# Start addresses of the buffers that TensorE reads: multiples of 256 bytes, and weight buffers 4128 bytes apart

## The chip, the cores and the metric
The kernel runs on one core of one Trainium2 chip. The metric is the device time of one execution in microseconds (us), of which the median of three runs is shown. A NeuronCore has TensorE (PE: matmuls, with a separate queue of weight loads, PEld), VectorE (DVE), ScalarE (ACT), GpSimd (POOL) and SyncE (SP, which here issues all the DMAs). On-chip memory (SBUF) has 128 partitions; an address below is a byte offset within each partition.

## The reference
Two layers on 256 tokens of width 1024, in fp32. A layer is a token mixer and a feed-forward block, each followed by a LayerNorm of `alpha * x + f(x)`.

```
proj = x @ w_in                      # x_rnn | g_rnn | q latent | kv latent | rope key | gate A | gate B
y_rnn = gelu(g_rnn) * rg_lru(causal_conv4(x_rnn))
y_mla = 16-head causal attention from the low-rank latents
x = layer_norm(alpha*x + (sigmoid(gateA)*y_rnn + sigmoid(gateB)*y_mla) @ w_out)
h_gate, h_val = split(causal_conv3(x @ w_up))          # 2 * 3072 columns
x = layer_norm(alpha*x + (gelu(h_gate) * h_val) @ w_down)
```

## The kernel before, in words
**Products.** A float32 matrix is split into a high part (`hi`, rounded to the type float32r by ScalarE, line 182) and a low rest (`lo`, the difference, by VectorE, line 183). `mm3` (lines 190 to 193) then makes one product of three matmuls: hi by hi, hi by lo, lo by hi. Each matmul has a stationary operand, brought in by a weight load of 128 columns (512 bytes per partition), and a moving operand, which streams through.

**Who is stationary and who moves.** In `proj_pair` (lines 515 to 528; all of x @ w_in but the latents, and x @ w_up from the third pair of columns on) the weights `wh`, `wl` are stationary and the activations `xhi`, `xlo` move, 256 columns (1024 bytes) at a time; 48 matmuls make one pair. `qps`, `kps`, `peps` and `gates` have the same shape and stationary `wh`, `wl`; the moving operand of `gates` are the tiles `xch`, `xcl`. In the down projection (`out_chunk` into `dacc`) and the output projection (into `oacc`) it is the other way round: activations (`hh`, `hl`; `mhi`, `mlo`) are stationary, weights (`wsh`, `wsl`; `wh`, `wl`) move, 512 columns at a time.

**Buffers.** `wpool` has 4 buffers `raw` of 8192 bytes, which the DMAs fill, and 6 each of `wh` and `wl` of 4096 bytes; `load_split` takes two of each per load, in rotation, so that successive loads use buffers 0 and 1, 2 and 3, 4 and 5. `big` has 19 buffers of 4096 bytes (`slot`), among them `xhi`, `xlo`, `mhi`, `mlo`, and the weights `wsh`, `wsl` of `load_split` with `in_slots`; and 4 of the residual. `sm` has 13 buffers of 1024 bytes (tag `k1`: `xch`, `xcl`, `hh`, `hl` and others) and 7 of 1536 (tag `k15`: the scores and the conv outputs), and small ones for statistics.

**Addresses.** Buffers are placed one after the other, pool by pool, at multiples of 32 bytes. By the allocated program `raw`, `wh`, `wl`, all slots and the residuals start 192 bytes past a multiple of 256; the `k1` tiles start on one; `k15` starts 96 past one, and the identity 128 past one. Slices used as operands start at further multiples of 512 bytes, but for the latent weights' second half (64 past one).

**Order.** The order on TensorE is written out: `ORDER` (lines 43 to 49) for the mixer, and the loops of `up` and `out_chunk` for the feed-forward, in which one `proj_pair` of 48 matmuls and one chunk of the down projection of 12 take turns. The other engines' order comes from a planner with issue-order edges (`behind`).

Of the kernel before, what the change touches and what calls it, by code (L numbers as in the profile page):

```python
# [11 lines left out]
F32 = mybir.dt.float32  # L12
# [5 lines left out]
P = 128  # L18
# [30 lines left out]
)  # L49
HELD = 4  # L50
WARM = 8
KORD = (0, 1, 4, 5, 2, 3, 6, 7)
NPAIR = DFF // P
ALPHA = (2 * DEPTH) ** 0.25
# [69 lines left out]
def trunk(ctx, tc, x_tok, x_chan, pos, wts, par, lnrow, consts, out):  # L124
# [4 lines left out]
    T = nc.tensor  # L129

    cpool = ctx.enter_context(tc.tile_pool(name="cpool", bufs=1))
    wpool = ctx.enter_context(tc.tile_pool(name="wpool", bufs=1))
    big = ctx.enter_context(tc.tile_pool(name="big", bufs=1))
    sm = ctx.enter_context(tc.tile_pool(name="sm", bufs=2))
    pp = ctx.enter_context(tc.tile_pool(name="pp", bufs=4, space=bass.MemoryType.PSUM))

    def slot(name, dt=F32):
        return big.tile([P, 1024], dt, tag="t4", name=name, bufs=19)

    def bank(name):  # L140
        return pp.tile([P, 512], F32, tag="pb", name=name)
# [3 lines left out]

    def load_raw(l, key, parts=None, between=None):
        o, n = WOFF[key]
        raw = wpool.tile([P, 2048], F32, tag="raw", name=f"raw{l}", bufs=4)
        src = wts[l, o:o + P * n].rearrange("(p n) -> p n", p=P)
        for i, (a, b) in enumerate(parts or ((0, n),)):  # L150
            if between and b == n:
                between()
            nc.sync.dma_start(out=raw[:, a:b], in_=src[:, a:b])
        return raw
# [11 lines left out]
    def load_split(l, key, cuts, in_slots=False, after=(None, None),  # L166
                   step=1024, parts=None, between=None):
        raw = load_raw(l, key, parts, between)
        if later[0]:
            after = ready[0]  # L170
        n = WOFF[key][1]
        res = []
        for a, b in cuts:
            if in_slots:
                hi, lo = slot("wsh", F32R), slot("wsl", F32R)
            else:
                hi = wpool.tile([P, 1024], F32R, tag="wh", name="wh", bufs=6)
                lo = wpool.tile([P, 1024], F32R, tag="wl", name="wl", bufs=6)
            for c in range(a, b, step):
                d = min(c + step, b)  # L180
                h, w = hi[:, c - a:d - a], raw[:, c:d]
                behind(A.activation(h, w, AF.Copy), after[0])  # L182
                lo_ins = V.tensor_tensor(out=lo[:, c - a:d - a], in0=w, in1=h.bitcast(F32),  # L183
                                         op=ALU.subtract)
                behind(lo_ins, after[1])
                last_split[0] = lo_ins
            res.append((hi, lo))
        return res
# [10 lines left out]
    ctx.enter_context(tc.manual_schedule(engines={mybir.EngineType.PE}))  # L199


    idle = cpool.tile([P, P], F32, name="idle")
    V.memset(idle, 0.0)
    spare = bank("spare")
    for _ in range(WARM):
# [26 lines left out]
        latw0.update(latent_weights(0, i, step=LATW if i > 1 else LH,  # L232
                                    parts=((0, LATW), (LATW, 2 * LATW))))

    ident = cpool.tile([P, P], F32, name="ident")
    make_identity(nc, ident)
    mask = cpool.tile([P, 2 * P], F32, name="mask")
    G.memset(mask, 0.0)
# [8 lines left out]
    for l in range(DEPTH):  # L247
# [3 lines left out]
    posi = cpool.tile([P, S], I32, name="posi")  # L251
    nc.sync.dma_start(out=posi, in_=pos[0:1, :].to_broadcast([P, S]))
    xres = [
        big.tile([P, D], F32, tag="xres", name=f"xres{t}", bufs=4) for t in range(NT)
    ]

    def pcol(l, name, i, n=1):
# [117 lines left out]
    class LayerNorm:  # L375
# [12 lines left out]

        def tile(self, t, accs):
            l, last = self.l, self.last  # L390
            z = big.tile([P, D], F32, tag="xres", name="z", bufs=4)
            st = sm.tile([P, 2, 6], F32, tag="st", name="st")
            mv = sm.tile([P, 2], F32, tag="mv", name="mv")
            rs = sm.tile([P, 1], F32, tag="rs", name="rs")
            hs = [slice(512 * h, 512 * h + 512) for h in range(2)]
            for h in range(2):
                V.scalar_tensor_tensor(
                    out=z[:, hs[h]], in0=self.xres[t][:, hs[h]], scalar=ALPHA, in1=accs[t][h],
                    op0=ALU.mult, op1=ALU.add,
                )  # L400
                V.bn_stats(st[:, h], z[:, hs[h]])
            V.bn_aggr(mv, st.rearrange("p a b -> p (a b)"))
            V.tensor_scalar(out=rs, in0=mv[:, 1:2], scalar1=EPS, scalar2=None, op0=ALU.add)
            G.tensor_tensor(out=rs, in0=rs, in1=nhalf[:, 0:1], op=ALU.pow)
            g, b = self.gb
            if last:
                for h in range(2):
                    V.scalar_tensor_tensor(out=z[:, hs[h]], in0=z[:, hs[h]], scalar=mv[:, 0:1],
                                           in1=g[:, hs[h]], op0=ALU.subtract, op1=ALU.mult)
                for h in range(2):  # L410
                    V.scalar_tensor_tensor(out=z[:, hs[h]], in0=z[:, hs[h]], scalar=rs,
                                           in1=b[:, hs[h]], op0=ALU.mult, op1=ALU.add)
                    nc.sync.dma_start(out=out[t * P:(t + 1) * P, hs[h]], in_=z[:, hs[h]])
                return
            nmr = sm.tile([P, 1], F32, tag="nmr", name="nmr")
            V.scalar_tensor_tensor(out=nmr, in0=mv[:, 0:1], scalar=-1.0, in1=rs,
                                   op0=ALU.mult, op1=ALU.mult)
            for c in (0, 256):
                V.tensor_scalar(out=z[:, c:c + 256], in0=z[:, c:c + 256], scalar1=mv[:, 0:1],
                                scalar2=rs, op0=ALU.subtract, op1=ALU.mult)  # L420
            A.activation(z[:, hs[1]], z[:, hs[1]], AF.Identity, scale=rs, bias=nmr)
            self.res.append(z)

        def turn(self, t):
# [8 lines left out]
            for cc in range(2):  # L433
                for q in range(2):
                    hi, lo = (v.rearrange("p (c s) -> p c s", c=4) for v in self.xs[q])
                    xt = sm.tile([P, 2, P], F32, tag="k1", name="lnx", bufs=13)
                    hv, lv = hi[:, 2 * cc:2 * cc + 2, ts], lo[:, 2 * cc:2 * cc + 2, ts]
                    for e in range(2):
                        c = 2 * cc + e
                        gc = pcol(l, self.gn, 4 * q + c)  # L440
                        bc = pcol(l, self.bn, 4 * q + c)
                        src = pts[q][:, c * P:(c + 1) * P]
                        if q == 0:
                            V.tensor_scalar(out=xt[:, e], in0=src, scalar1=gc, scalar2=bc,
                                            op0=ALU.mult, op1=ALU.add)
                        else:
                            behind(A.activation(xt[:, e], src, AF.Identity, scale=gc, bias=bc),
                                   ea)
                    ea = A.activation(hv, xt, AF.Copy)
                    ev = V.tensor_tensor(out=lv, in0=xt, in1=hv.bitcast(F32), op=ALU.subtract)  # L450
# [30 lines left out]
    def lat_evac(l, t):  # L481
# [2 lines left out]
            A.activation(lt[:, h * LH:(h + 1) * LH], lacc[t][h][:, :LH], AF.Copy)  # L484
        lat.append(lt)
        sq = slot("sq")
        ms = sm.tile([P, 2], F32, tag="ms", name="ms")
        A.activation(sq[:, :QL], lt[:, :QL], AF.Square, scale=QL ** -0.5,
                     accum_out=ms[:, 0:1])
        A.activation(sq[:, QL:QL + KVL], lt[:, QL:QL + KVL], AF.Square,  # L490
# [17 lines left out]
    for l in range(DEPTH):  # L508
# [83 lines left out]
        def conv_branch(i):  # L592
            ps = proj_pair(("x", i))
            for m in range(2):
# [5 lines left out]
                for k in range(1, 4):  # L600
# [1 line left out]
                        out=dst[:, k:], in0=src[:, :S - k], scalar=pcol(l, "cw", 8 * (3 - k) + c),  # L602
                        in1=dst[:, k:], op0=ALU.mult, op1=ALU.add,
                    ))
                xh = sm.tile([P, S], F32R, tag="k1", name="xch", bufs=13)
                xl = sm.tile([P, S], F32R, tag="k1", name="xcl", bufs=13)
                A.activation(xh, dst, AF.Copy)
                V.tensor_tensor(out=xl, in0=dst, in1=xh.bitcast(F32), op=ALU.subtract)
                xsp[c] = (xh, xl)
# [136 lines left out]
        def scores(c):  # L746
            g, pr = divmod(c, 2)
            _, q96, k96 = qk[g]
            rsum = sm.tile([P, 2, 2], F32, tag="rsum", name="rsum", bufs=3)
            sns = []  # L750
            for hh in range(2):
                h4 = 2 * pr + hh
# [2 lines left out]
                         start=True, stop=True)  # L755
                T.matmul(sps[:, P:P + S], lhsT=q96[:, h4, P:], rhs=k96[:, h4],  # L756
                         start=True, stop=True)
                sn = sm.tile([P, 3 * P], F32, tag="k15", name="sn", bufs=7)
                nm = sm.tile([P, 2], F32, tag="nm", name="nm", bufs=4)
                V.tensor_tensor_reduce(sn[:, :P], sps[:, :P], mask[:, P:], -1.0, 3e38,  # L760
                                       ALU.add, ALU.min, nm[:, 0:1])
                er = V.tensor_tensor_reduce(sn[:, P:], sps[:, P:3 * P], mask, -1.0, 3e38,
# [14 lines left out]
        def flip(c):  # L777
            sns = pst[c]
            pts = []
            for hh in range(2):  # L780
                ptp = bank("ptp")
                for b in range(3):
                    T.transpose(ptp[:, b * P:(b + 1) * P], sns[hh][:, b * P:(b + 1) * P], ident)  # L783
                pT = sm.tile([P, 3 * P], F32, tag="k15", name="pT", bufs=7)
                A.activation(pT, ptp[:, :3 * P], AF.Copy)
                pts.append(pT)
            pst[c] = pts

        def values(c):
# [10 lines left out]
            if mer[c // 4] is None:  # L800
                mer[c // 4] = (slot("mhi", F32R), slot("mlo", F32R))
            cs = slice((c % 4) * S, (c % 4) * S + S)
            mg = sm.tile([P, S], F32, tag="k1", name="mg", bufs=13)
            V.tensor_tensor(out=mg, in0=yps[:, :S], in1=sB[c // 4][:, cs], op=ALU.mult)
            V.tensor_tensor(out=mg, in0=mg, in1=r_t[c // 4][:, cs], op=ALU.add)
            split2(mer[c // 4][0][:, cs], mer[c // 4][1][:, cs], mg)
# [76 lines left out]
        def up(j):  # L883
# [8 lines left out]
            for m in range(2):  # L892
                ch = m * NPAIR + j
                src = ps[:, m * S:(m + 1) * S]
                dst = sm.tile([P, S], F32, tag="k15", name=f"u{m}", bufs=7)
                ea = A.activation(dst, src, AF.Identity, scale=pcol(l, "fw", 96 + ch),  # L896
                                  bias=pcol(l, "fb", ch))
                for k in range(1, 3):
# [6 lines left out]
            convs.append((ea, ev))  # L905
            A.activation(u[0], u[0], AF.Gelu_apprx_tanh)
            V.tensor_tensor(out=u[1], in0=u[1], in1=u[0], op=ALU.mult)  # L907
            mh = sm.tile([P, S], F32R, tag="k1", name="hh", bufs=13)
            ml = sm.tile([P, S], F32R, tag="k1", name="hl", bufs=13)
            split2(mh, ml, u[1])  # L910
            hq[j] = (mh, ml)

# [145 lines left out]
```

## Time and profile before
| | |
|---|---|
| median of 3 runs | 804.9 us (804.83 to 805.35) |
| profiled execution, its own time | 804.24 us |
| its span, first to last instruction | 802.4 us |
| mean granted TensorE clock | 0.997 of full |
| busy: PE, PEld, DVE, ACT | 791.0, 741.2, 650.5, 509.1 us |

The span is that of one execution. A matmul's listed duration includes the time that it takes to pass through the array and overlaps its successors, so busy times of PE say little; the distance from one matmul's start to the next one's (its pitch below) is what a stream of them costs. Start times in the timeline are given to 0.01 us, so a pitch is read over many matmuls.

### The profile page before, as it was taken

What the parts mean: (1) busy time and instruction counts of PE and PEld (TensorE: products, weight loads), DVE (VectorE), ACT (ScalarE), POOL (GpSimd) and SP (SyncE); (2) the same over time, 40 slices, a digit from 0 to 9 for tenths busy, and PEclk for the clock granted to TensorE, in tenths of its full rate; (3) what the DMA queues carried; (4) which work ended last, traced back from release to release, by engine and by line L of the source; (5) the groups of instructions that cost most, each with busy time, mean ns of one, the idle gap of its engine ahead of it and who ended that gap; (6) DMA issues with size and microseconds to landing.
All of it is one profiled execution on the core that took longest, in us unless ns stands there. A gap on an engine that the chain in (4) does not pass through costs nothing.

```text
span 802.4 us, 14518 instructions
## 1 busy us (share of the span) xinstructions
PE 791.0 (99%) x5712; PEld 741.2 (92%) x5712; DVE 650.5 (81%) x1260; ACT 509.1 (63%) x910; POOL 10.9 (1%) x27
## 2 busy tenths in 40 slices
PE   9999999999999999999999999999999999999996
PEld 8999899878999999999899999998799999999994
DVE  6998889997699977667777886999887998677755
ACT  5765987783777465556475579688567665555540
POOL 1000000000000000000000000000000000000000
PEclk9999999999999999999999999999999999999998
DMA  8955436524356655435625544563524756655311
GB/s 313 344 185 211 152 115 242 187 85 181 158 210 263 210 177 209 174 122 218 236 79 201 183 169 139 173 219 121 208 76 184 276 196 211 210 165 203 106 53 53
DMA packets 26468, 144.76 MB, mean 180 GB/s; under 512 B 3360, under 2 KB 7072, under 8 KB 11808
## 3 DMA queue, kind: packets, MB, share of 16 engines
q1 hardware_dynamic: 26400, 143.84, 50.6%
q8 instruction: 45, 0.74, 0.4%
q14 instruction: 23, 0.19, 0.1%
HBM read 140.68 MB, written 1.05 MB: 177 GB/s over the span
## 4 chain that ended last, share of the span: by engine, by line
PE 97%; DMA 1%; DVE 1%; ACT 1%; SPq 0%; issue 0%; DVEq 0%
PE proj L193 18%; PE proj L191 18%; PE proj L192 18%; PE dacc L191 6%; PE dacc L192 6%; PE dacc L193 6%; PE oacc L191 2%; PE oacc L192 2%; PE oacc L193 2%; PE sps L756 2%; PE yps L797 2%; PE ptp L783 1%; PE latp L192 1%; PE latp L193 1%; PE latp L191 1%; PE sps L754 1%
## 5 line engine op out<-in xcount | busy, mean ns | idle before, releaser
L193 PE MATMUL proj<-xhi,wl 128*128 128x256 f32 x1216 | 344.2, 283 | 0.1
L191 PE MATMUL proj<-xhi,wh 128*128 128x256 f32 x1216 | 344.1, 283 | 0.0
L192 PE MATMUL proj<-xlo,wh 128*128 128x256 f32 x1216 | 343.6, 283 | 0.0
L183 DVE TENSOR_TENSOR wl<-raw,wh 128x1024 fp32r<-128x1024 f32 (+5 forms) x226 | 241.9, 1089 | 50.4 <-ACT wh L182 49.9
L182 ACT ACTIVATE wh<-raw 128x1024 fp32r<-128x1024 f32 (+5 forms) x226 | 208.7, 952 | 103.0 <-PE proj L192 88.4
L192 PEld LDWEIGHTS proj<-xlo,wh 128*128 128x128 f32 x1216 | 232.9, 192 | 1.7
L191 PEld LDWEIGHTS proj<-xhi,wh 128*128 128x128 f32 x1216 | 232.9, 192 | 1.6
L193 PEld LDWEIGHTS proj<-xhi,wl 128*128 128x128 f32 x1216 | 232.9, 192 | 0.7 <-DVE wl L183 0.7
L899 DVE SCALAR_TENSOR_TENSOR u<-proj,par,u 128x255 f32<-128x255 f32 (+1 forms) x176 | 83.5, 479 | 39.2 <-ACT u L896 37.1
L896 ACT ACTIVATE u<-proj,par 128x256 f32<-128x256 f32 x88 | 49.1, 558 | 94.0 <-DVE u L899 71.5
L191 PE MATMUL dacc<-wsh,hh 128*128 128x512 f32 x192 | 76.2, 397 | 0.0
L192 PE MATMUL dacc<-wsl,hh 128*128 128x512 f32 x192 | 75.9, 395 | 0.0
L193 PE MATMUL dacc<-wsh,hl 128*128 128x512 f32 x192 | 75.9, 395 | 0.0
L183 DVE TENSOR_TENSOR wsl<-raw,wsh 128x1024 fp32r<-128x1024 f32 (+2 forms) x66 | 69.8, 1077 | 0.0
L182 ACT ACTIVATE wsh<-raw 128x1024 fp32r<-128x1024 f32 (+2 forms) x66 | 59.7, 937 | 0.0
L193 PEld LDWEIGHTS dacc<-wsh,hl 128*128 128x128 f32 x192 | 36.1, 188 | 8.9
L191 PEld LDWEIGHTS dacc<-wsh,hh 128*128 128x128 f32 x192 | 36.2, 189 | 7.0
L192 PEld LDWEIGHTS dacc<-wsl,hh 128*128 128x128 f32 x192 | 36.1, 188 | 6.9
L196 ACT ACTIVATE hh<-u 128x256 fp32r<-128x256 f32 x48 | 19.6, 408 | 13.7 <-DVE u L907 13.7
L191 PE MATMUL oacc<-wh,mhi 128*128 128x512 f32 x64 | 26.6, 415 | 0.0
L192 PE MATMUL oacc<-wl,mhi 128*128 128x512 f32 x64 | 25.0, 391 | 0.0
L193 PE MATMUL oacc<-wh,mlo 128*128 128x512 f32 x64 | 25.0, 391 | 0.0
(213 smaller groups left out, 1132.2 us busy)
## 6 DMA issues: line engine op xcount, KB each, us to landing
raw<-in_wts SPq DMA_DIRECT2D x114, 1024.0 KB, 4.9
raw<-in_wts SPq DMA_DIRECT2D x8, 832.0 KB, 4.9
gb<-in_lnrow SPq DMA_DIRECT2D x8, 512.0 KB, 8.0
raw<-in_wts SPq DMA_DIRECT2D x4, 672.0 KB, 4.1
raw<-in_wts SPq DMA_DIRECT2D x7, 336.0 KB, 6.6
raw<-in_wts SPq DMA_DIRECT2D x4, 512.0 KB, 4.5
xres<-in_x_tok SPq DMA_DIRECT2D x2, 512.0 KB, 6.0
k<-krot SPq DMA_DIRECT2D x8, 128.0 KB, 2.4
```

What stands on the lines that cost most here:

```text
L182: behind(A.activation(h, w, AF.Copy), after[0])
L183: lo_ins = V.tensor_tensor(out=lo[:, c - a:d - a], in0=w, in1=h.bitcast(F32), op=ALU.subtract)
L191: T.matmul(o, lhsT=lh, rhs=rh, start=start, stop=False)
L192: T.matmul(o, lhsT=lh, rhs=rl, start=False, stop=False)
L193: T.matmul(o, lhsT=ll, rhs=rh, start=False, stop=stop)
L196: A.activation(hi, src, AF.Copy)
L754: T.matmul(sps[:, :P], lhsT=q96[:, h4, :P], rhs=k96[:, h4, :P], start=True, stop=True)
L756: T.matmul(sps[:, P:P + S], lhsT=q96[:, h4, P:], rhs=k96[:, h4], start=True, stop=True)
L783: T.transpose(ptp[:, b * P:(b + 1) * P], sns[hh][:, b * P:(b + 1) * P], ident)
L797: T.matmul(yps[hh * 64:hh * 64 + 64, t * P:S], lhsT=vs[:, hv:hv + 64], rhs=pts[hh][:, 2 * t * P:(2 + t) * P], start=t == 0, stop=t == 1)
L896: ea = A.activation(dst, src, AF.Identity, scale=pcol(l, "fw", 96 + ch), bias=pcol(l, "fb", ch))
L899: ev = V.scalar_tensor_tensor(out=dst[:, k:], in0=src[:, :S - k], scalar=pcol(l, "fw", 48 * (2 - k) + ch), in1=dst[:, k:], op0=ALU.mult, o ...
```

## The change
Tiles that TensorE reads ask for a start at a multiple of `LINE` = 256 bytes. The split weights `wh` and `wl` ask for none, but their buffers are made `STEP` = 8 elements (32 bytes) longer and used without that end, so that each starts 4128 bytes after the one before. The statistics' tiles move from `sm` to a pool of their own, `tiny`, ahead of `wpool`. No instruction is added, removed or reordered in the text, and no number of buffers changes.

```diff
+LINE = 256
+STEP = 8
...
+    tiny = ctx.enter_context(tc.tile_pool(name="tiny", bufs=2))
     wpool = ctx.enter_context(tc.tile_pool(name="wpool", bufs=1))
...
     def slot(name, dt=F32):
-        return big.tile([P, 1024], dt, tag="t4", name=name, bufs=19)
+        return big.tile([P, 1024], dt, tag="t4", name=name, bufs=19, align_bytes=LINE)
...
-        raw = wpool.tile([P, 2048], F32, tag="raw", name=f"raw{l}", bufs=4)
+        raw = wpool.tile([P, 2048], F32, tag="raw", name=f"raw{l}", bufs=4, align_bytes=LINE)
...
-                hi = wpool.tile([P, 1024], F32R, tag="wh", name="wh", bufs=6)
-                lo = wpool.tile([P, 1024], F32R, tag="wl", name="wl", bufs=6)
+                hi = wpool.tile([P, 1024 + STEP], F32R, tag="wh", name="wh", bufs=6)[:, :1024]
+                lo = wpool.tile([P, 1024 + STEP], F32R, tag="wl", name="wl", bufs=6)[:, :1024]
...
-    idle = cpool.tile([P, P], F32, name="idle")
+    idle = cpool.tile([P, P], F32, name="idle", align_bytes=LINE)
...
-            st = sm.tile([P, 2, 6], F32, tag="st", name="st")
+            st = tiny.tile([P, 2, 6], F32, tag="st", name="st")
...
-            mh = sm.tile([P, S], F32R, tag="k1", name="hh", bufs=13)
+            mh = sm.tile([P, S], F32R, tag="k1", name="hh", bufs=13, align_bytes=LINE)
```

The same `align_bytes=LINE` is given to `ident`, the residuals, and every other tile of the tags `k1` and `k15`; `mv`, `rs`, `nmr`, `ms`, `rsum` and `nm` go to `tiny` as `st` does.

## Rows read from the trace of the kernel before

**Rows 1.** The page: busy time by engine; granted TensorE clock in 40 slices.
```profile
PE 791.0 (99%) x5712; PEld 741.2 (92%) x5712; DVE 650.5 (81%) x1260; ACT 509.1 (63%) x910; POOL 10.9 (1%) x27
...
PEclk9999999999999999999999999999999999999998
```

**Rows 2.** The page: chain that ended last, shares of the span by engine.
```profile
PE 97%; DMA 1%; DVE 1%; ACT 1%; SPq 0%; issue 0%; DVEq 0%
```

**Rows 3.** Waits of PE: line, releaser, total us, times, longest us.
```profile
PE spare L206 <- DVE lruw L334: 1.1, 1, 1.1
PE gates L192 <- DVE xcl L608: 1.0, 1, 1.0
PE gates L191 <- ACT xch L607: 0.8, 1, 0.8
PE latp L191 <- ACT wh L182: 0.6, 2, 0.3
```

**Rows 4.** Groups by form: out<-moving and stationary, count, busy us, mean ns, idle before.
```profile
L193 PE MATMUL proj<-xhi,wl 128*128 128x256 f32 x1216 | 344.2, 283 | 0.1
L191 PE MATMUL proj<-xhi,wh 128*128 128x256 f32 x1216 | 344.1, 283 | 0.0
L192 PE MATMUL proj<-xlo,wh 128*128 128x256 f32 x1216 | 343.6, 283 | 0.0
...
L191 PE MATMUL dacc<-wsh,hh 128*128 128x512 f32 x192 | 76.2, 397 | 0.0
...
L191 PE MATMUL oacc<-wh,mhi 128*128 128x512 f32 x64 | 26.6, 415 | 0.0
...
L191 PE MATMUL qps<-lth,wh 128*128 128x256 f32 x48 | 14.3, 297 | 0.0
...
L191 PE MATMUL kps<-lth,wh 128*128 128x256 f32 x32 | 9.8, 305 | 0.0
...
L191 PE MATMUL peps<-lth,wh 128*128 128x256 f32 x24 | 7.2, 298 | 0.0
```

**Rows 5.** Timeline of PE: start us, us, instruction; first and 97th of a run of proj.
```profile
94.54 0.28 PE L191 MATMUL proj<-xhi,wh 128*128 128x256 f32 x1
...
106.06 0.28 PE L191 MATMUL proj<-xhi,wh 128*128 128x256 f32 x1
```

**Rows 6.** Timeline of PE: first and 18th of a run of gates.
```profile
83.61 0.28 PE L191 MATMUL gates<-xch,wh 128*128 128x256 f32 x1
...
85.62 0.28 PE L193 MATMUL gates<-xch,wl 128*128 128x256 f32 x1
```

**Rows 7.** Timeline of PE: last proj, first of 12 dacc, and the first proj behind.
```profile
290.32 0.28 PE L193 MATMUL proj<-xhi,wl 128*128 128x256 f32 x1
290.44 0.40 PE L191 MATMUL dacc<-wsh,hh 128*128 128x512 f32 x1
...
293.25 0.28 PE L191 MATMUL proj<-xhi,wh 128*128 128x256 f32 x1
293.36 0.27 PE L192 MATMUL proj<-xlo,wh 128*128 128x256 f32 x1
293.48 0.28 PE L193 MATMUL proj<-xhi,wl 128*128 128x256 f32 x1
293.59 0.28 PE L191 MATMUL proj<-xhi,wh 128*128 128x256 f32 x1
```

**Rows 8.** Timeline of PE: first and 13th of a run of oacc.
```profile
187.11 0.39 PE L193 MATMUL oacc<-wh,mlo 128*128 128x512 f32 x1
...
189.83 0.39 PE L193 MATMUL oacc<-wh,mlo 128*128 128x512 f32 x1
```

**Rows 9.** Busy us by stretch: PE, PEld, DVE, ACT, POOL; clock, DMA share, GB/s.
```profile
79.00:89.00 10.00, 8.19 (x66) 7.79 (x66) 9.02 (x17) 9.97 (x22) 0.00 (x0) 1.00 0.31 110
109.00:119.00 10.00, 10.00 (x84) 9.86 (x83) 10.00 (x9) 8.23 (x12) 0.00 (x0) 1.00 0.19 51
```

**Rows 10.** Timeline of PEld: one weight load that waited, and for whom.
```profile
119.11 0.19 PEld L193 LDWEIGHTS proj<-xhi,wl 128*128 128x128 f32 x1 [0.25 <-DVE wl L183]
```

**Rows 11.** Groups by form of ACT: the split into slots and into wh.
```profile
L182 ACT ACTIVATE wh<-raw 128x1024 fp32r<-128x1024 f32 x160 | 165.5, 1059 | 86.8 <-PE proj L192 78.1 <-issue 5.2 <-DVE lruw L337 1.4
...
L182 ACT ACTIVATE wsh<-raw 128x1024 fp32r<-128x1024 f32 x48 | 49.0, 1049 | 0.0
```

More of the change, by code (lines that the diff above doesn't have):

```diff
@@ L233, in trunk @@
                                     parts=((0, LATW), (LATW, 2 * LATW))))
-    ident = cpool.tile([P, P], F32, name="ident")
+    ident = cpool.tile([P, P], F32, name="ident", align_bytes=LINE)
     make_identity(nc, ident)
@@ L253, in trunk @@
     xres = [
-        big.tile([P, D], F32, tag="xres", name=f"xres{t}", bufs=4) for t in range(NT)
+        big.tile([P, D], F32, tag="xres", name=f"xres{t}", bufs=4, align_bytes=LINE) for t in range(NT)
     ]
@@ L390, in tile @@
             l, last = self.l, self.last
-            z = big.tile([P, D], F32, tag="xres", name="z", bufs=4)
-            st = sm.tile([P, 2, 6], F32, tag="st", name="st")
-            mv = sm.tile([P, 2], F32, tag="mv", name="mv")
-            rs = sm.tile([P, 1], F32, tag="rs", name="rs")
+            z = big.tile([P, D], F32, tag="xres", name="z", bufs=4, align_bytes=LINE)
+            st = tiny.tile([P, 2, 6], F32, tag="st", name="st")
+            mv = tiny.tile([P, 2], F32, tag="mv", name="mv")
+            rs = tiny.tile([P, 1], F32, tag="rs", name="rs")
             hs = [slice(512 * h, 512 * h + 512) for h in range(2)]
@@ L414, in tile @@
                 return
-            nmr = sm.tile([P, 1], F32, tag="nmr", name="nmr")
+            nmr = tiny.tile([P, 1], F32, tag="nmr", name="nmr")
             V.scalar_tensor_tensor(out=nmr, in0=mv[:, 0:1], scalar=-1.0, in1=rs,
@@ L435, in turn @@
                     hi, lo = (v.rearrange("p (c s) -> p c s", c=4) for v in self.xs[q])
-                    xt = sm.tile([P, 2, P], F32, tag="k1", name="lnx", bufs=13)
+                    xt = sm.tile([P, 2, P], F32, tag="k1", name="lnx", bufs=13, align_bytes=LINE)
                     hv, lv = hi[:, 2 * cc:2 * cc + 2, ts], lo[:, 2 * cc:2 * cc + 2, ts]
@@ L486, in lat_evac @@
         sq = slot("sq")
-        ms = sm.tile([P, 2], F32, tag="ms", name="ms")
+        ms = tiny.tile([P, 2], F32, tag="ms", name="ms")
         A.activation(sq[:, :QL], lt[:, :QL], AF.Square, scale=QL ** -0.5,
@@ L604, in conv_branch @@
                     ))
-                xh = sm.tile([P, S], F32R, tag="k1", name="xch", bufs=13)
-                xl = sm.tile([P, S], F32R, tag="k1", name="xcl", bufs=13)
+                xh = sm.tile([P, S], F32R, tag="k1", name="xch", bufs=13, align_bytes=LINE)
+                xl = sm.tile([P, S], F32R, tag="k1", name="xcl", bufs=13, align_bytes=LINE)
                 A.activation(xh, dst, AF.Copy)
@@ L748, in scores @@
             _, q96, k96 = qk[g]
-            rsum = sm.tile([P, 2, 2], F32, tag="rsum", name="rsum", bufs=3)
+            rsum = tiny.tile([P, 2, 2], F32, tag="rsum", name="rsum", bufs=3)
             sns = []
@@ L757, in scores @@
                          start=True, stop=True)
-                sn = sm.tile([P, 3 * P], F32, tag="k15", name="sn", bufs=7)
-                nm = sm.tile([P, 2], F32, tag="nm", name="nm", bufs=4)
+                sn = sm.tile([P, 3 * P], F32, tag="k15", name="sn", bufs=7,
+                             align_bytes=LINE)
+                nm = tiny.tile([P, 2], F32, tag="nm", name="nm", bufs=4)
                 V.tensor_tensor_reduce(sn[:, :P], sps[:, :P], mask[:, P:], -1.0, 3e38,
@@ L783, in flip @@
                     T.transpose(ptp[:, b * P:(b + 1) * P], sns[hh][:, b * P:(b + 1) * P], ident)
-                pT = sm.tile([P, 3 * P], F32, tag="k15", name="pT", bufs=7)
+                pT = sm.tile([P, 3 * P], F32, tag="k15", name="pT", bufs=7,
+                             align_bytes=LINE)
                 A.activation(pT, ptp[:, :3 * P], AF.Copy)
@@ L802, in values @@
             cs = slice((c % 4) * S, (c % 4) * S + S)
-            mg = sm.tile([P, S], F32, tag="k1", name="mg", bufs=13)
+            mg = sm.tile([P, S], F32, tag="k1", name="mg", bufs=13, align_bytes=LINE)
             V.tensor_tensor(out=mg, in0=yps[:, :S], in1=sB[c // 4][:, cs], op=ALU.mult)
@@ L894, in up @@
                 src = ps[:, m * S:(m + 1) * S]
-                dst = sm.tile([P, S], F32, tag="k15", name=f"u{m}", bufs=7)
+                dst = sm.tile([P, S], F32, tag="k15", name=f"u{m}", bufs=7,
+                              align_bytes=LINE)
                 ea = A.activation(dst, src, AF.Identity, scale=pcol(l, "fw", 96 + ch),
@@ L907, in up @@
             V.tensor_tensor(out=u[1], in0=u[1], in1=u[0], op=ALU.mult)
-            mh = sm.tile([P, S], F32R, tag="k1", name="hh", bufs=13)
-            ml = sm.tile([P, S], F32R, tag="k1", name="hl", bufs=13)
+            mh = sm.tile([P, S], F32R, tag="k1", name="hh", bufs=13, align_bytes=LINE)
+            ml = sm.tile([P, S], F32R, tag="k1", name="hl", bufs=13, align_bytes=LINE)
             split2(mh, ml, u[1])
```

## The prediction
> **What bounds the kernel now.** I read the busy times first: PE 99%, with the granted clock at full in every slice but the last [rows 1]. Then the chain that ended last: 97% of it is PE [rows 2]. Then PE's waits: 3.5 us in all, of which 1.8 lie in one place, the recurrent gates of the first layer [rows 3]. So the end is set by how closely TensorE's instructions follow one another, and by little else. The groups say which: 3648 matmuls `proj` of 256 columns, 576 `dacc` and 192 `oacc` of 512 (three lines of each, one of them shown for the last two) [rows 4]. Their mean durations don't help, since they overlap. The timeline does. From 94.54 to 106.06 us 96 `proj` follow one another in 11.52 us: a pitch of 120.0 ns [rows 5]. A pitch of 120 ns times 3648 is 438 us, more than half the span.
>
> What decides about this change is whether that pitch hangs on addresses, and three places answer. `gates` has the shape of `proj` and the same stationary buffers (192 past a multiple of 256), but its moving tiles start on the multiple. 17 pitches take 2.01 us: 118.2 ns, 118.0 without the first one, which still follows a `proj` [rows 6]. `oacc` has both operands 192 past: 12 pitches in 2.72 us, 226.7 ns [rows 8]. `dacc` has the same shape as `oacc`, but its stationary tiles start on the multiple, 64 bytes ahead of the moving ones: 12 in 2.81 us, 233.9 ns [rows 7]. No wait stands between any of them. So the same shape costs other times at other relative starts of the two operands, and the differences are 2 and 7 ns per matmul.
>
> A second reading: equal starts give 120.0 at 256 columns, and 226.7 at 512. The 256 columns more cost 106.7, so both carry 13.3 ns that don't grow with the length: a cost per weight load. At unequal starts it is 11.3 (`gates`) and 20.6 (`dacc`). The first three `proj` behind a `dacc` take 0.34 us [rows 7], 113 ns each, or up to 117 by the rounding of the two starts (I use 115), before the 120 of the long run is reached: the 120 is a state into which a run of equal starts falls, not the least that the shape allows.
>
> **One rule of the notes speaks against all this.** The rows: 120.0 against 118.0 ns for one shape, with PE waiting for nobody [rows 3, 5, 6]. The Trainium skill, "SBUF — State Buffer", section "Who interferes with whom", gives PE two read ports of its own, one for the moving operand and one for weight loads, and says "PE and ACT never wait on anyone". By that rule no start address changes a pitch, and the time would stay at 804.9. The trace does not agree for these pairs of streams, by 2 and 7 ns; the rule is the third rival below, with a small chance.
>
> **The change, part by part.** It adds and removes no instruction, DMA or wait, so every term is a pitch times a count.
>
> (1) `proj`, 3648. Moving tiles go to multiples of 256. `raw` ends on one, so the six `wh` start 0, 32, 64, 96, 128 and 160 past one, and the six `wl` 192, 224, 0, 32, 64 and 96. Two of three weight loads are `wh`, one is `wl`, and almost none has equal starts with its neighbours any more. Rows exist for two unequal relations only: 192 (`gates`, 2.0 ns less than equal starts) and 64 (`dacc`, 7.2 ns more, at 512 columns). At 256 columns 64 ahead stands in one pitch, that of the last `proj` with the first weights of `dacc` loaded beside it: 290.32 to 290.44, 120 ns or a little less [rows 7], so not 7 ns more. The bounds are -5 ns (the 115 behind a `dacc`) and +7.2 ns. I take -2.0, the value of `gates`, as the only long run of this shape with unequal starts: -7.3 us. (2) `qps`, `kps`, `peps`, 312 of the same shape (three lines each [rows 4]): -0.6 us by the same 2.0. `gates` itself goes from one unequal relation to others: 0.
>
> (3) `dacc`, 576: both operands now start on multiples, equal as in `oacc`. At most 7.2 ns each, 4.1 us; but chunks have 12 matmuls, and a run comes to its steady pitch only behind several, as the `proj` behind `dacc` show. Between 2.4 and 4.1, I take -3.2 us. (4) `oacc`, 192: stationary slots on multiples, moving `wh`, `wl` now 0 to 224 past: the equal starts are lost. At 7.2 ns on the two thirds that run steadily: +0.9 us. The latents have mixed starts before and after; `upt` keeps equal ones: 0, by up to 1 us either way.
>
> (5) What the others take back. PE can gain only where its inputs are there. At 85 us the first layer's `gates` wait for ACT and DVE, while ACT is busy 9.97 of 10 us [rows 3, 9]. Ten `proj_pair`, 480 matmuls, run ahead of it by `ORDER`; their 1.0 us turns into a longer wait there. At 119 us a weight load waits for DVE's split, with DVE busy for all of the 10 us before [rows 9, 10]; the 240 `proj` ahead of it lose their 0.5 us, in both layers. So +2.0 us. In the feed-forward nothing of this kind shows among PE's waits.
>
> (6) The splits write to buffers with other starts. ACT took 1059 ns into `wh` and 1049 into slots [rows 11]: 10 ns either way on 160 splits is 1.6 us of ACT, hidden by PE, which ACT idled for 78.1 us before these very splits; were the cover gone it would be at most those 1.6. DMAs get other targets; they hold 1% of the chain [rows 2].
>
> Sum: -7.3 - 0.6 - 3.2 + 0.9 + 2.0 = -8.2 us, on the profiled execution's own 804.24: 796.0. The median of the runs is 0.7 above it, so **796.7 us**.
>
> **The rivals.**
> First, **slower: weights ahead of the moving stream cost what `dacc` pays.** If the 7.2 ns of 64 bytes ahead hold at 256 columns for 32 to 160 ahead, then five of six `wh` pay (6.0 ns on average) and three of six `wl` do (3.6, less 0.7 for the two at 192 and 224): (2 x 6.0 + 2.9) / 3 = 5.0 ns on 3960 matmuls, +19.8, and with terms 3 and 4 +17.5: 822. With half the price it is +7.6: 812.5, which is what I take. It decides from where the mean over the twelve starts is 1.0 ns above 120 (3.9 us, which pay terms 3 and 4 and 0.2%). For it: `dacc` against `oacc`, the larger of the two differences. Against it: the one pitch at 290.32.
> Second, **only `dacc` gains**: `proj` settles at 120 at whatever starts. -3.2 + 0.9: 802.6. For it: 120.0 is exactly the same for the first and second half of a pair, 512 bytes apart. Against it: `gates` stays at 118.
> Third, **nothing moves**: 804.9. The differences would belong to the pools or the PSUM tiles, not to the starts; `gates` and `dacc` are the two whose operands lie in `sm`.
> Fourth, **the 120 breaks for good** and 115 lasts: -5.0 on 3960, -19.8, with -2.3 for terms 3 and 4 and 4 taken back: 786.8. For it: the three pitches at 293.25; against it: they rise again within ten.
> A floor below that stands in the Trainium skill, "TensorE: Matmul & The Clock Gate", section "Back-to-back issue gap": columns over 2.4 plus 2.5 ns, an estimate of 109.2 for this shape, by which the full -10.8 ns on 3960 matmuls would be -43 us. No run of this shape here comes near it.
>
> **How the numbers follow.** Main case 0.45: 796.7, its own range 791 to 802, since 1 ns on `proj` is 3.6 us. Slower 0.27: 812.5, 806 to 822. Only `dacc` 0.11: 802.6. Nothing 0.09: 804.9. The lasting 115 0.08: 786.8. The range 785 to 814 leaves out the upper third of the slower case and the lower part of the last, not quite 2 in 10. What a measurement can tell from no change is 0.2%, 1.6 us: faster 0.63, same 0.10, slower 0.27.
>
> **What would show it.** Right: a long run of `proj` at 117 to 119 ns in the timeline, not the same for the three pairs of buffers; `dacc` falling from 233.9 towards 227; `oacc` rising; longer waits at `gates` and before the wait for DVE's `wl`. Wrong: `proj` at 120.0 still (second or third rival), or above 121 in the pairs with `wh` 64 to 160 past (first).

## The result, and the profile after

The changed kernel took 796.1 us (median of 4 runs, 795.5 to 796.3) against 805.1 in the same series: a ratio of 0.9887, 95% interval 0.9871 to 0.9903. Forecast were 796.7, with 791 to 802 as the main case's own range. The profiled execution took 796.0 us, its span 794.2 against 802.4.

The page after: busy time by engine, then the shares of the chain that ended last, which answer to [rows 1, 2].

```profile
PE 781.1 (98%) x5712; PEld 733.8 (92%) x5712; DVE 649.7 (82%) x1260; ACT 508.8 (64%) x910; POOL 10.9 (1%) x27
...
PE 89%; ACT 4%; DVE 3%; DMA 1%; issue 1%; SPq 0%; POOL 0%; DVEq 0%
```

The same instructions take less of PE, and 7% of the span now lies with ACT and DVE on the chain, where 2% did. The timeline of PE after, first the same stretch of 96 `proj` as in [rows 5]:

```profile
93.76 0.28 PE L194 MATMUL proj<-xhi,wh 128*128 128x256 f32 x1
...
105.14 0.28 PE L194 MATMUL proj<-xhi,wh 128*128 128x256 f32 x1
```

and a feed-forward chunk: the 12th and the last `proj` of a pair, then the first and last of 12 `dacc`.

```profile
292.38 0.28 PE L196 MATMUL proj<-xhi,wl 128*128 128x256 f32 x1
...
296.62 0.28 PE L196 MATMUL proj<-xhi,wl 128*128 128x256 f32 x1
296.74 0.40 PE L194 MATMUL dacc<-wsh,hh 128*128 128x512 f32 x1
...
299.24 0.39 PE L196 MATMUL dacc<-wsh,hl 128*128 128x512 f32 x1
```

96 pitches in 11.38 us are 118.5 ns, 36 in 4.24 us are 117.8, where 120.0 stood. Eleven pitches of `dacc` in 2.50 us are 227.3, where 12 took 233.8 each (2.805 us by the unrounded starts of [rows 7]; the prediction has 233.9). `oacc`, the run of [rows 8], has lost its 226.7: 12 pitches in 2.79 us are 232.5.

```profile
186.42 0.39 PE L194 MATMUL oacc<-wh,mhi 128*128 128x512 f32 x1
...
189.21 0.39 PE L194 MATMUL oacc<-wh,mhi 128*128 128x512 f32 x1
```

What waits after. First PE's waits (line, releaser, total us, times, longest), then two weight loads and whom they waited for:

```profile
PE proj L196 <- DVE wl L186: 1.3, 3, 0.5
PE spare L209 <- DVE lruw L337: 1.1, 1, 1.1
PE latp L194 <- ACT wh L185: 1.0, 1, 1.0
PE gates L195 <- DVE xcl L611: 1.0, 1, 1.0
PE gates L194 <- ACT xch L610: 1.0, 1, 1.0
```
```profile
118.32 0.19 PEld L196 LDWEIGHTS proj<-xhi,wl 128*128 128x128 f32 x1 [0.62 <-DVE wl L186]
...
507.48 0.19 PEld L196 LDWEIGHTS proj<-xhi,wl 128*128 128x128 f32 x1 [0.65 <-DVE wl L186]
```

The wait for DVE's `wl` at 119 us [rows 10] is the same one, 0.62 instead of 0.25 us, and its twin in the second layer is at 507, with 0.65 instead of 0.24. The splits themselves didn't move: by form, ACT takes 1061 and 1049 ns, as against 1059 and 1049 [rows 11].

```profile
L185 ACT ACTIVATE wh<-raw 128x1024 fp32r<-128x1024 f32 x160 | 165.7, 1061 | 81.5 <-PE proj L195 72.1 <-issue 5.0 <-DMA raw<-in_wts 2.2
...
L185 ACT ACTIVATE wsh<-raw 128x1024 fp32r<-128x1024 f32 x48 | 49.1, 1049 | 0.0
```

### The profile page after: what moved, and what is told of

The parts are those of the page before. It is cut to its first block, busy times and chain, and to the rows that moved or that the text cites. A ratio compares the mean times of both kernels' runs of the same rounds, so it can differ in the third digit from the quotient of the medians.

```text
span 794.2 us, 14518 instructions
## 1 busy us (share of the span) xinstructions
PE 781.1 (98%) x5712; PEld 733.8 (92%) x5712; DVE 649.7 (82%) x1260; ACT 508.8 (64%) x910; POOL 10.9 (1%) x27
## 4 chain that ended last, share of the span: by engine, by line
PE 89%; ACT 4%; DVE 3%; DMA 1%; issue 1%; SPq 0%; POOL 0%; DVEq 0%
PE proj L196 16%; PE proj L195 16%; PE proj L194 16%; PE dacc L195 6%; PE dacc L194 6%; PE dacc L196 6%; PE oacc L194 2%; PE oacc L196 2%; PE oacc L195 2%; PE sps L759 2%; PE yps L802 2%; PE ptp L787 1%; PE sps L757 1%; PE upt L196 1%; PE upt L194 1%
## 5 line engine op out<-in xcount | busy, mean ns | idle before, releaser
L196 PEld LDWEIGHTS proj<-xhi,wl 128*128 128x128 f32 x1216 | 229.0, 188 | 1.9 <-DVE wl L186 1.9
L194 PEld LDWEIGHTS proj<-xhi,wh 128*128 128x128 f32 x1216 | 229.1, 188 | 1.4
L195 PEld LDWEIGHTS proj<-xlo,wh 128*128 128x128 f32 x1216 | 228.7, 188 | 1.4
```

Of the source, the lines that this page charges most:

```text
L194: T.matmul(o, lhsT=lh, rhs=rh, start=start, stop=False)
L195: T.matmul(o, lhsT=lh, rhs=rl, start=False, stop=False)
L196: T.matmul(o, lhsT=ll, rhs=rh, start=False, stop=stop)
```

## The experiments

Twelve kernels, each with a series of the kernel before beside it (medians 803.7 to 804.4). "Past" below is the start of the 12 `wh` and `wl` in bytes past a multiple of 256; the moving operands lie on a multiple unless it is said otherwise. A pitch is read from two starts in the timeline; totals over a group are summed over all of its starts.

**Which property of the addresses is it?** Three edits of the changed kernel replace the 32-byte steps by one constant start, with a pad tile ahead of `wh` (64 bytes: 0 past; 128 bytes: 64 past). Without a pad they land 192 past, since they ask for no alignment: that kernel is the change without its steps. The pad tile, here and below, adds one short memset on GpSimd.

```diff
-STEP = 8
+STEP = 0
+PADH = 16
...
-                hi = wpool.tile([P, 1024 + STEP], F32R, tag="wh", name="wh", bufs=6)[:, :1024]
+                if PADH and "ph" not in pads:
+                    pads["ph"] = wpool.tile([P, PADH], F32, tag="ph", name="ph", bufs=1)
+                    G.memset(pads["ph"][:], 0.0)
+                hi = wpool.tile([P, 1024], F32R, tag="wh", name="wh", bufs=6)
...
```

`PADH` counts elements of 4 bytes: 16 puts `wh` and `wl` on a multiple, 32 puts them 64 past, 0 leaves the pad out. `wl` gets its 1024 columns in the same way, directly behind `wh`.

> Edit to the changed kernel: no 32-byte steps; a pad tile puts all 12 wh and wl on a multiple of 256, as everything else is, so moving and stationary start equal in every stream. Theory A (what counts is the start of the stationary operand relative to the moving one, modulo 256; equal starts lock at 120.0 and 226.7 ns): proj 120.0, dacc 226.7, oacc 226.7; only dacc's 3.0 us remain of the 9.0: 802. Theory B (what counts is that the moving operand starts on a multiple of 256, as gates had it before): proj 118.0, time as changed, 796. Theory C (successive weight loads must differ in start): proj 120.0, 802, as A.

Measured: 802.3 us, ratio 0.9973 (0.9963 to 0.9982). The timeline of PE, `gates` and then the long run of `proj`:

```profile
69.35 0.28 PE L204 MATMUL gates<-xch,wh 128*128 128x256 f32 x1
...
70.67 0.28 PE L206 MATMUL gates<-xch,wl 128*128 128x256 f32 x1
...
96.16 0.28 PE L204 MATMUL proj<-xhi,wh 128*128 128x256 f32 x1
...
107.68 0.28 PE L204 MATMUL proj<-xhi,wh 128*128 128x256 f32 x1
```

Eleven pitches of `gates` in 1.32 us: 120.0, where 118.0 stood before [rows 6]; `proj` 11.52 us for 96, 120.0 as before. With equal starts `gates` gets the 120 too, with its moving tiles on the multiple in both kernels. Theory B falls, A stands. Equal starts everywhere take 2.9 us off `dacc`, summed over its starts, and 2.1 off the time.

> Edit to the changed kernel: no steps; all wh and wl 192 past a multiple of 256, moving operands on it: one constant relation, that of gates before. A: proj 118.0, dacc 226.7, oacc (whose moving operand is wh, wl, so its stationary one is 64 ahead, as in dacc before) 233.7, +0.9 us on that: 796 to 797. B: 118.0 and 796. C: proj locks again at 120.0: 802 to 803.

Measured: 792.7 us (789.9 to 794.3), ratio 0.9860 (0.9841 to 0.9879): 3 us under what any theory gave, and faster than with the steps.

> Edit to the changed kernel: no steps; all wh and wl 64 past a multiple of 256, moving operands on it: the relation that dacc had before at 512 columns. The rival 'slower' of the prediction: proj at 120 + 7.2 = 127 ns on 3960 matmuls, +28 us, 830. A in the form that any unequal start breaks the lock: proj 117 to 119, 796. B: 118.0, 796. C: 120.0, 802.

Measured: 789.8 us (788.5 to 790.7), ratio 0.9816 (0.9799 to 0.9833): faster than the change itself. The timeline, 96 `proj` of the mixer and 36 of the feed-forward:

```profile
93.07 0.28 PE L204 MATMUL proj<-xhi,wh 128*128 128x256 f32 x1
...
103.95 0.28 PE L204 MATMUL proj<-xhi,wh 128*128 128x256 f32 x1
...
290.29 0.28 PE L206 MATMUL proj<-xhi,wl 128*128 128x256 f32 x1
...
294.53 0.28 PE L206 MATMUL proj<-xhi,wl 128*128 128x256 f32 x1
```

10.88 us over 96 are 113.3 ns, 4.24 over 36 are 117.8. Both are steady (the single pitches repeat as 114, 113, 113 and as 118, 118, 117), and the kernel at 192 past has the same two, in most places the same one. So the prediction's "slower" is refuted where it was priced, at 64; theory C falls, since all the loads start alike; and one pair of starts has two steady pitches.

The other part alone, the steps without the alignment, in the kernel before:

```diff
+STEP = 8
...
-                hi = wpool.tile([P, 1024], F32R, tag="wh", name="wh", bufs=6)
+                hi = wpool.tile([P, 1024 + STEP], F32R, tag="wh", name="wh", bufs=6)[:, :1024]
```
(and `wl` likewise)

> Edit to the kernel before: only the 32-byte steps of wh and wl, no alignment. Moving operands lie 64 past a multiple of 256 (slots), wh 0 to 224 past one in steps of 32, dacc keeps its relation of 64. A: proj 118, dacc 233.7 as before, oacc somewhat up: 805.1 - 5.3 - 0.5 + 0.5 = 799.5 to 800. B: nothing lies on a multiple, proj 120: 805. C: proj 118: 800.

Measured: 799.4 us, ratio 0.9938 (0.9922 to 0.9954), as A and C have it. The timeline, 36 `proj`, then 12 `dacc`:

```profile
292.32 0.28 PE L194 MATMUL proj<-xhi,wl 128*128 128x256 f32 x1
...
296.58 0.28 PE L194 MATMUL proj<-xhi,wl 128*128 128x256 f32 x1
296.69 0.40 PE L192 MATMUL dacc<-wsh,hh 128*128 128x512 f32 x1
...
299.26 0.39 PE L194 MATMUL dacc<-wsh,hl 128*128 128x512 f32 x1
```

`proj` takes 118.3 ns with its moving operands 64 past a multiple of 256; `dacc`, whose relation is kept, 233.6. The steps alone and equal starts for `dacc` account for most of the change: 0.9938 times 0.9973 is 0.9911, against 0.9887 for both, with intervals of 0.0010 to 0.0016 either way on each of the three. The rest, 0.0024 or 1.9 us, is about as large as these intervals together.

**Is any unequal start as good?** The same edit at the other starts (`PADH` 24, 40, 48, 56, 8).

> As the kernel with all wh and wl 64 past a multiple of 256, but 32 past one. Two runs with constant unequal starts (192 and 64) showed two steady pitches, 113.3 in most of the mixer and 117.8 in the feed-forward, and 120.0 nowhere. Theory E (any unequal start breaks the 120): proj at 113.3 or 117.8 again, 788 to 796. Theory D (starts count in units of 64 bytes): 32 is as good as equal, 120.0, 802.

> As before, 96 past a multiple of 256. D and E: 113.3 or 117.8, 788 to 796. Open, and asked of this run: whether the feed-forward, which locked at 117.8 at 64 and at 192, locks at 113.3 at another start; that would be 4.5 ns on 2112 matmuls, 9.5 us less: 780.

> As before, 128 past a multiple of 256: half of the period that the addresses seem to have. Theories D and E: 113.3 or 117.8, 788 to 796. Theory F (the period is 128 bytes): equal again, 120.0, 802.

> All wh and wl 160 past a multiple of 256. So far: 0 gave 120.0; 32: 118.3; 64: 113.3 and 117.8; 96: 117.3 and 118.7; 128: 118.6 and 120.0; 192: 113.3 and 117.8; 224: 116.7 and 117.8. If 160 lies between its neighbours: 117 to 119, 794 to 799; nothing under 117.

> As before, 224 past a multiple of 256, that is 32 short of the next. E: 113.3 or 117.8, 788 to 796. D, with starts rounded to 64 bytes: as 192, 790 to 794. If the sign of the difference decides, with 32 and 224 as its two sides, their steady pitches differ.

| past | `proj` in the mixer, ns | in the feed-forward, ns | us | ratio |
|---|---|---|---|---|
| 0 | 120.0 | 120.0 | 802.3 | 0.9973 (0.9963 to 0.9982) |
| 32 | 118.3 | 118.3 | 798.6 | 0.9925 (0.9896 to 0.9954) |
| 64 | 113.3 | 117.8 | 789.8 | 0.9816 (0.9799 to 0.9833) |
| 96 | 118.7 | 117.3 | 795.8 | 0.9891 (0.9862 to 0.9919) |
| 128 | 118.7 | 120.0 | 802.1 | 0.9981 (0.9970 to 0.9993) |
| 160 | 120.0 | 120.0 | 804.5 | 1.0000 (0.9987 to 1.0013) |
| 192 | 113.3 | 117.8 | 792.7 | 0.9860 (0.9841 to 0.9879) |
| 224 | 116.7, 117.8 | 116.7 | 792.2 | 0.9846 (0.9817 to 0.9874) |

E is wrong: 160 past is unequal and as slow as equal. The timeline of that kernel, 36 `proj` of the feed-forward in 4.32 us, 120.0:

```profile
295.81 0.28 PE L206 MATMUL proj<-xhi,wl 128*128 128x256 f32 x1
...
300.13 0.28 PE L206 MATMUL proj<-xhi,wl 128*128 128x256 f32 x1
```

D is wrong too, since 32 is better than 0, and F half wrong: at 128 the feed-forward is at 120.0 and the mixer is not. The run at 160 was expected between its neighbours, at 117 to 119, and missed that too. The open question of the run at 96 got a no: the pairs of `proj` between the chunks of `dacc`, most of the feed-forward, are at 113.3 at none of the eight starts. And 32 and 224, the same distance on either side of equal, differ (118.3 against 116.7), so the sign counts. Each start has one or two levels of its own, one of them in most of the mixer and one in most of the feed-forward (the table has these); none of the eight is above 120.0.

**What chooses between two steady pitches?** In the kernel with `wh` and `wl` 64 past, the small tiles, `hh` and `hl` with them, move 64 as well, by a pad tile at the head of `sm`:

```diff
+    kpad = sm.tile([P, 16], F32, tag="kpad", name="kpad", bufs=1)
+    G.memset(kpad[:], 0.0)
...
-            mh = sm.tile([P, S], F32R, tag="k1", name="hh", bufs=13, align_bytes=LINE)
+            mh = sm.tile([P, S], F32R, tag="k1", name="hh", bufs=13)
```
(and every other tile of `k1` and `k15`)

> The kernel with all wh and wl 64 past a multiple of 256, and now the tiles of 1024 and 1536 bytes (hh, hl, xch, xcl, scores) 64 past one as well. proj keeps its starts; dacc gets the relation that it had before (stationary 64 ahead), gates gets equal starts. All theories on addresses: dacc 226.7 to about 233.7, +4.0 us; gates 113.4 to 120.0. Theory G (which of its two steady pitches a stretch of proj falls into is set by how it is entered, that is by the dacc ahead of it): proj of the feed-forward may leave 117.8 for 113.3, -9.5 us: 784. Theory H (the pitch belongs to the two starts and the buffers alone): proj in the feed-forward stays at 117.8: 794.

Measured: 786.2 us, ratio 0.9781 (0.9753 to 0.9810). The timeline, 36 `proj` in 4.08 us and the `dacc` behind them:

```profile
289.58 0.28 PE L209 MATMUL proj<-xhi,wl 128*128 128x256 f32 x1
...
293.66 0.28 PE L209 MATMUL proj<-xhi,wl 128*128 128x256 f32 x1
293.77 0.39 PE L207 MATMUL dacc<-wsh,hh 128*128 128x512 f32 x1
...
296.33 0.40 PE L209 MATMUL dacc<-wsh,hl 128*128 128x512 f32 x1
```

`proj`, whose addresses and starts are unchanged, went from 117.8 to 113.3 ns; `dacc` went from 229.2 to 232.7 over these 11. H falls: a pitch does not belong to the two starts and the buffers alone. G says what the run showed, that a change ahead of a stretch can move it to its other pitch. That the `dacc` ahead did it is not shown by itself, since the tiles that ACT and DVE write beside `proj` moved by 64 bytes too. Nor does G settle every stretch: in this kernel the run of 144 `proj` that opens the feed-forward, behind the same `upf` with the same relations, takes 113.3 in the first layer (from 211 us) and 117.8 in the second (from 594).

**A mixed pair of starts.** `wh` 64 and `wl` 192 past, with a second pad between them, and then the same relations without any alignment:

```diff
-STEP = 8
+STEP = 0
+PADH = 32
+PADL = 32
```

> As the kernel with all wh and wl 64 past a multiple of 256, but wl 192 past. Alone, 64 and 192 gave the same two steady pitches. H: 113.3 in the mixer and 117.8 in the feed-forward again, 789 to 793. A rival: a change of start between successive loads, as the 32-byte steps have it, keeps the stream from the 113.3: 117 to 119 everywhere, 796.

Measured: 781.1 us (779.7 and 782.4), ratio 0.9718 (0.9676 to 0.9759). Both readings were wrong, on the good side. The timeline of the feed-forward:

```profile
286.18 0.28 PE L206 MATMUL proj<-xhi,wl 128*128 128x256 f32 x1
...
290.26 0.28 PE L206 MATMUL proj<-xhi,wl 128*128 128x256 f32 x1
290.37 0.40 PE L204 MATMUL dacc<-wsh,hh 128*128 128x512 f32 x1
...
292.89 0.39 PE L206 MATMUL dacc<-wsh,hl 128*128 128x512 f32 x1
```

`proj` is at 113.3 behind a `dacc` that keeps its equal starts, after a first few of 114 to 122 in every chunk; the mixer is at 113.3 too. Summed over all of its starts, `proj` takes 418.2 us instead of 438.0, though it waits more:

```profile
PE proj L206 <- DVE wl L196: 2.8, 2, 1.4
PE spare L219 <- DVE lruw L347: 1.1, 1, 1.1
PE gates L204 <- ACT xch L620: 1.0, 1, 1.0
PE gates L205 <- DVE xcl L621: 1.0, 1, 1.0
```

> Edit to the kernel before, without any alignment and without steps: three pad tiles (32, 128 and 64 bytes) move the buffers so that no operand of proj lies on a multiple of 256 (xhi, xlo 160 past one, wh 224, wl 96), but wh is 64 and wl 192 past the moving operand, as in the kernel with wh at 64 and wl at 192. dacc keeps its relation of 64. If only the relation between the two operands counts: proj 113.3, dacc 233.7 as before, gates (now equal for wh) up: 781 + 3.0 + 0.5 = 784.5, within 2. If the place within 256 bytes counts as well, proj is elsewhere, 117 to 120: 795 to 805.

Measured: 784.0 us (782.8 to 784.3), ratio 0.9751 (0.9735 to 0.9768). The timeline, 96 `proj` in 10.88 us:

```profile
90.87 0.28 PE L201 MATMUL proj<-xhi,wh 128*128 128x256 f32 x1
...
101.75 0.28 PE L201 MATMUL proj<-xhi,wh 128*128 128x256 f32 x1
```

113.3 again, with moving operands 160, `wh` 224 and `wl` 96 past. Equal starts gave 120.0 both at 192 past (the kernel before) and on the multiple. What counts is the start of the stationary operand relative to the moving one, not the multiple of 256.

## Why the prediction was right, point by point

The distances between successive starts of PE, summed by group over both traces (their total falls by 8.2 us, as the span does):

| term | predicted, us | measured, us |
|---|---|---|
| (1) `proj`, pitch alone | -7.3 | -6.6 |
| (2) `qps`, `kps`, `peps` | -0.6 | -0.5 |
| (3) `dacc` | -3.2 | -3.0 |
| (4) `oacc` | +0.9 | +0.5 |
| (5) taken back: `proj` and `gates` waiting | +2.0 | +1.4 |
| latents, `vps`, all others | 0 | 0.0 |
| sum | -8.2 | -8.2 |

That the sums agree to a tenth is luck: the gains in (1), (2) and (3) came out 1.0 us smaller than forecast, the losses in (4) and (5) 1.0 us smaller as well.

**What bounds it.** Right: PE at its pitch bounds the kernel, and three pads of 224 bytes together, which move addresses and add three short memsets on GpSimd, took 19.7 us off 803.7 in the last experiment.

**(1), (2).** The size, -2.0 ns, came close (-6.6 us are 1.8 ns), by luck in part, since its source was poorer than it looked. The prediction took `gates` at 118.0 [rows 6] as what unequal starts cost. In the kernel at 192 past, with the same pair of starts, `gates` ran at 113.4, 23 pitches in 2.61 us:

```profile
469.27 0.28 PE L204 MATMUL gates<-xch,wh 128*128 128x256 f32 x1
...
471.88 0.28 PE L206 MATMUL gates<-xch,wl 128*128 128x256 f32 x1
```

So the 118 was one of two steady pitches. The changed kernel doesn't settle at all; nine in ten of its single pitches lie between 115 and 121, with a mean of 117.9 (and of 117.7, 117.9 and 118.2 in turn in the first layer's feed-forward, by the three pairs of buffers, as forecast), and the plain mean of the eight constant kernels' `proj` is 118.0. That the steps average over the starts fits both numbers and wasn't shown by itself. The second reading, that the 120 is a state into which a run falls, was right, and truer than the prediction made use of.

The list of starts in (1) is wrong, though -2.0 doesn't hang on it. By the allocated program `wh` begins 192 bytes past the multiple on which `raw` ends, as the kernel without steps and without a pad shows too. So the six `wh` start 192, 224, 0, 32, 64 and 96 past, and the six `wl` 128, 160, 192, 224, 0 and 32. What hangs on the list is the price of "slower": 32 to 160 ahead then holds for three of six `wh` and three of six `wl`, 2.9 ns in the mean instead of 5.0, which makes 814 us at the full price instead of 822.

**(3).** Right: equal starts give the 226.7 of `oacc` at another place within the 256 bytes, and the entry costs the first pitches of a chunk. The steps alone left `dacc` at 233.6.

**(4).** Right in sign; the mean rose by 2.7 ns a matmul instead of 4.8.

**(5).** Right at the two waits for DVE's `wl`, +0.4 each where 0.5 was forecast. Wrong at `gates`, +0.2 instead of +1.0. The last `gates` before its wait started 0.9 us earlier (84.71 instead of 85.62), but the one that waited for ACT's `xch` started 0.7 us earlier too (first before, then after):

```profile
86.71 0.38 PE L191 MATMUL gates<-xch,wh 128*128 128x256 f32 x1 [0.82 <-ACT xch L607]
```
```profile
85.97 0.39 PE L194 MATMUL gates<-xch,wh 128*128 128x256 f32 x1 [0.99 <-ACT xch L610]
```

The prediction held ACT's delivery fixed in time; it moved ahead with PE. And it had not named a third wait for `wl`, at 22 us, where the first weights are split: 0.67 instead of 0.19, +0.5. So the +1.4 near the +2.0 hides two errors of opposite sign. In the fastest kernel the two waits for `wl` have grown to 1.4 each, the largest of PE's waits there.

**(6).** Right: 2 ns on the split into `wh`, none on that into slots.

**The rivals.** "Slower" had the larger of the two differences for it, and fell for the reason that the one pitch at 290.32 gave: what 64 ahead costs at 512 columns it doesn't cost at 256. "Only `dacc` gains" is what the kernel with equal starts everywhere does, 802.3 against the rival's 802.6. "Nothing moves" fell with the pitches. For it stood the Trainium skill, "SBUF — State Buffer", section "Who interferes with whom", with "PE and ACT never wait on anyone": here the pitch of one shape runs from 113.3 to 120.0 ns with nothing but start addresses moved, so the rule is not the whole of it for PE's own two streams; by what these hold each other up, no run shows. "The 120 breaks for good" didn't come with this change and did with constant starts: the 115 was no accident of three pitches. The 109.2 that the prediction calls a floor is an estimate from the Trainium skill, "TensorE: Matmul & The Clock Gate", section "Back-to-back issue gap", by the formula that it gives for the gap of a single matmul in isolation. No run reached it; the least steady pitch here, with a weight load for every matmul, is 113.3.

**Left open.** Why 64 and 192 past have the 113.3 and 160 has 120.0, and why `wh` and `wl` at different starts reach it behind any `dacc`, no run explains. No run moves the writes of ACT and DVE into these tiles by themselves; they moved with the reads. The series at 192 past spreads over 4.4 us where those of the kernel before spread over 0.9 to 2.3. Its four runs fall in the order of their granted clocks (789.9 us at 0.997, 792.4 at 0.995, 793.0 and 794.3 at 0.994), so part of the spread can be stretches at half clock, as the last section has one. Whether stretches also take another of their steady pitches from one execution to the next is open: of each kernel one execution was traced.

## What to carry to other kernels

Where TensorE is the bound, read its pitch from the starts in the timeline, by shape, and compare streams of one shape: a difference without a wait can come from addresses, as it did here. Set the start of the stationary buffers relative to the moving ones, with pads of 32 bytes or more, and measure the few relations that there are: here `wh` 64 and `wl` 192 past took 6.7 ns off the steady pitch of `proj`, and a multiple of 256 for every buffer, which makes the starts equal, took none. Steps that spread the starts bought about the mean of the relations here, not the best of them, and a stretch can have a second pitch that one relation alone does not rule out.

## What the runs showed of the hardware that was not expected

- A stream of one shape at one pair of starts has more than one steady pitch (113.3 and 117.8 ns at 64 past), and can keep the one it fell into over a whole run of 240 matmuls.
- The best relation belongs to the shape: 64 ahead gives 113.3 at 256 columns, in `proj`, and at 512, in `dacc`, costs 7 ns against equal starts, 233.8 [rows 7] against 226.7 [rows 8].
- A wait can be followed by a stretch at half clock, and the wait's length doesn't tell whether. Here is the kernel at 64 past around the waits at `gates`, and then the kernel at 192 past in the same stretches (us; busy us of PE, PEld, DVE, ACT, POOL; granted clock, DMA share, GB/s):

```profile
82.00:84.50 2.50, 1.31 (x7) 0.92 (x7) 2.49 (x5) 2.50 (x5) 0.00 (x0) 1.00 0.23 95
84.50:86.40 1.90, 1.07 (x5) 1.07 (x6) 1.90 (x4) 1.90 (x6) 0.00 (x0) 0.75 0.00 0
86.50:88.60 2.10, 2.10 (x11) 2.10 (x11) 1.49 (x5) 2.10 (x5) 0.00 (x0) 0.50 0.56 114
```
```profile
82.00:84.50 2.50, 0.89 (x6) 0.48 (x4) 2.50 (x4) 2.50 (x5) 0.00 (x0) 1.00 0.07 30
84.50:86.40 1.90, 1.51 (x13) 1.52 (x14) 1.90 (x3) 1.90 (x6) 0.00 (x0) 1.00 0.00 0
86.50:88.60 2.10, 2.10 (x21) 2.10 (x20) 1.49 (x5) 2.10 (x4) 0.00 (x0) 1.00 0.78 197
```

  In the first, PE was busy for 1.31 of 2.50 and 1.07 of 1.90 us, and the clock fell; 11 `proj` then ran at the 1.2 GHz level (0.50), which cost these 11 about 1.1 us (213 ns each instead of 113). In the second, PE was busy for the same 2.4 us of the 4.4, with two distances of 2.66 us together at that place, and the clock stayed at 1.00 (2.4 GHz). In the kernel with equal starts everywhere it fell behind two distances of only 2.43 us. What decides it, these traces don't show.
